# Roots on GpSimd, last squares summed by TensorE, and three kinds of work moved from GpSimd to VectorE

## The chip, the cores and the metric

The kernel runs on one core of one Trainium2 chip. The metric is the device time of that core in microseconds (us), as the median of several executions. The core's engines work side by side, each through a queue of its own in a fixed order: TensorE (PE, matrix products and transposes; PEld is its loading of weights), VectorE (DVE), ScalarE (ACT), GpSimd (POOL) and SyncE (SP, which issues the transfers). An engine that waits for another holds up everything that stands behind the waiting instruction in its queue.

## The reference

Two transformer blocks run one after the other on 256 tokens of width 1024. The second block, which the change touches, has two layers of three sub-layers each (feed-forward, mixer, feed-forward) for two streams: the tokens `h` and a context `hc` of 256 rows, which falls away after the second layer's mixer has read it.

```python
def rms_norm(x, g):
    y = xf * lax.rsqrt(jnp.mean(xf * xf, axis=-1, keepdims=True) + EPS)
    return y.astype(x.dtype) * g
...
    def pre(t, mm, i, gi):
        return rms_norm(t, g[gi]) * (1 + mm[:, :, i + 1]) + mm[:, :, i]

    def post(t, y, mm, i, gi, wres):
        return t + wres * mm[:, :, i + 2] * rms_norm(y, g[gi])

    h = post(h, swiglu(pre(h, m, 0, 0), ffn_wi[0], ffn_wo[0]), m, 0, 1, 0.5)
    hc = post(hc, swiglu(pre(hc, mc, 0, 0), ffn_wi[0], ffn_wo[0]), mc, 0, 1, 0.5)
    u = pre(h, m, 3, 2)
    uc = pre(hc, mc, 3, 2)
```

So between two sub-layers stand two root mean squares: one over the output y, one over the stream after y was added. The first block (a recurrent mixer, a differential attention and two mixtures of experts) is not touched.

## The kernel before

Activations lie transposed: a stream is 8 tiles of 128 channels by 256 tokens (`xT`, `ctxT`). Every product of the second block is made of three TensorE products of halves (`mm3`: high by high, high by low, low by high), so each operand is split into `hi` (ScalarE copy) and `lo` (VectorE subtraction); weights are split as they arrive from memory (`raw`, `hi`, `lo` in `chunks`), inputs in `split_sum`.

A sub-layer ends with 8 output tiles y (index d) per stream. `Output.add` writes for each three squares or products (y squared, gated y squared, gated y by x) into one tile of 128 by 3 by 256: the first is `acc`, the later ones are `ysq`. The tiles d = 1 to 5 are added to `acc` by GpSimd, d = 6 by VectorE, and `acc` and the last tile are then summed over channels by TensorE with a matrix of ones (`sums`, into `st`). `Output.rows` turns `st` into per-token columns (a copy `rowsums`, two TensorE transposes into `tp`, a copy `sums`), and takes the first reciprocal root (`rstd`: a bit trick and two polynomial steps, 11 VectorE instructions on 128 by 2 elements, `rs_x` to `rs_y`). From it and the three sums it works out the squares of the new stream without waiting for it, and takes the second root. Each root is spread over all partitions by two TensorE transposes (`row`). `update` then adds y to the stream (one VectorE product `xs`, one GpSimd addition per tile) and makes the next inputs `u`: a VectorE product, a ScalarE `hi`, and for even tiles a VectorE `lo`, for odd tiles a second ScalarE pass and a GpSimd `lo`.

There are five such boundaries in the second block: after the first feed-forward, the mixer and the second feed-forward of layer 0 and after the first feed-forward of layer 1 for both streams (stream 0 first, stream 1 after it), and after the mixer of layer 1 for stream 0 alone. The last sub-layer (`ffn_last`) has tokens as rows, and takes a root per half of the tokens at the very end. The mixers read a bias, which GpSimd turns round in place (12 subtractions of 128 by 256 per layer).

The code is written in the order of the sub-layers; a scheduler sets the order of each engine's queue from it, so that instructions of stream 1's output, stream 0's update and the next sub-layer stand interleaved.

Of the kernel before, what the change touches and what calls it, by code (L numbers as in the profile page):

```python
# [18 lines left out]
D = 1024  # L19
KT = 8  # L20
# [11 lines left out]
READY = 2  # L32

# [201 lines left out]
class Kernel:  # L235
# [117 lines left out]
    def split_sum(self, hi, lo, src, col, by_pool=False):  # L353

        nc = self.nc
        if by_pool:
            nc.scalar.activation(src, src, AF.Identity, bias=col)
            nc.scalar.activation(hi, src, AF.Copy)
            nc.gpsimd.tensor_sub(lo, src, hi)  # L359
        else:  # L360
            nc.scalar.activation(hi, src, AF.Identity, bias=col)  # L361
            nc.vector.scalar_tensor_tensor(lo, src, col, hi, op0=ALU.add, op1=ALU.subtract)
# [43 lines left out]
    def rstd(self, pool, st, n, dim, tag):  # L406
# [15 lines left out]
        nc.vector.scalar_tensor_tensor(y, t, 1.5, y, op0=ALU.add, op1=ALU.mult)  # L422
        return y
# [54 lines left out]
    class Output:  # L478
# [10 lines left out]
        def add(self, d, s):  # L489
# [10 lines left out]
            if 0 < d < KT - 1:  # L500
                (nc.vector if d == KT - 2 else nc.gpsimd).tensor_add(self.acc[s], self.acc[s], t)  # L501
# [30 lines left out]
        def rows(self, s):  # L532

            kern, nc, pool = self.kern, self.kern.nc, self.pool
            v = pool.tile([128, 3, 2], F32, tag="sums", name="sums", bufs=2)
            t = pool.tile([128, S], F32, tag="xs", name="rowsums", bufs=kern.xs_bufs)[:96]
            nc.vector.tensor_copy(t, self.st[:96, s * S:s * S + S])
# [3 lines left out]
            nc.vector.tensor_copy(v, tp.rearrange("p (j q c) -> p q j c", j=2, q=3)[:, :, :, 0])  # L541
            y2, z2, xz = (v[:, q] for q in range(3))
            x2 = pool.tile([128, 2], F32, tag=f"x2_{s}", name="x2", bufs=2)
            r1 = kern.rstd(pool, y2, 2, D, "n")
            rb1 = kern.row(r1)
            nc.vector.tensor_mul(z2, z2, r1)
            nc.vector.scalar_tensor_tensor(z2, xz, 2.0, z2, op0=ALU.mult, op1=ALU.add)
            nc.vector.tensor_mul(z2, z2, r1)
            nc.vector.tensor_add(x2, self.x2[s], z2)
            self.x2[s] = x2  # L550
            return rb1, kern.row(kern.rstd(pool, x2, 2, D, "n2"))

    def update(self, pool, u, s, out, gs, sh):
# [12 lines left out]
        for k in range(KT):  # L566
# [3 lines left out]
            self.split_sum(u[:, k, 0], u[:, k, 1], t, sh[:, k:k + 1], k % 2)  # L570
# [313 lines left out]
    def mix(self, ring, pool, l, u, out, u_home, proj_home):  # L884
# [974 lines left out]
```

## Time and profile before

| | |
|---|---|
| median of 3 runs | 2648.66 us (2643.46 to 2649.74) |
| the profiled execution's own time | 2648.6 us |
| its span in the trace | 2646.8 us |
| mean granted clock of TensorE | 0.969 |
| busy: PE, PEld, DVE, ACT, POOL | 93%, 72%, 61%, 33%, 13% of the span |
| chain that ended last | PE 58%, DVE 7%, ACT 1%, POOL 0% |

A row of a timeline or a group names the line of the kernel, the engine, the operation and its tiles (out<-in, buffer numbers left out), its size, and in brackets how long the engine sat idle before it and whose end released it. The granted clock is a share of TensorE's full speed of 2.4 GHz; its other level is 1.2 GHz, 0.5. The first block takes about the first 840 us of the span, the second the rest.

### The profile page before, as it was taken

How to read it: one execution, taken by the hardware profiler on the slowest of the kernel's cores; microseconds unless marked ns; L12 is line 12 of the kernel's file. 1: busy time of each engine (PE TensorE's matmuls, PEld its weight loads, DVE VectorE, ACT ScalarE, POOL GpSimd, SP SyncE). 2: the span in 40 equal slices, each digit the busy share in tenths (PEclk: the TensorE clock that was granted, in tenths of full speed). 3: DMA queues.
4: the chain of work that ended last, by engine and by line, in shares of the span. 5: the costliest groups of instructions: out<-in, count | busy, mean ns of one | idle time of the engine just before them, and what ended most of it. 6: DMA issues, size and time to landing. Idle time of an engine off the chain costs nothing.

```text
span 2646.8 us, 38413 instructions
## 1 busy us (share of the span) xinstructions
PE 2457.4 (93%) x14614; PEld 1899.9 (72%) x14614; DVE 1620.8 (61%) x3515; ACT 881.5 (33%) x1547; POOL 340.5 (13%) x364
## 2 busy tenths in 40 slices
PE   4989898988988999998999899999899999898998
PEld 4864344775443888887876788888788888776997
DVE  7873214884131676738847868664868645958555
ACT  3430003551011332224337432223422223455543
POOL 0010000110000000004236500001400002434000
PEclk9989998998999999999999999999999999998999
DMA  9889996789997365622521147443156533322553
GB/s 333 303 351 408 420 419 259 295 292 370 398 410 314 128 199 163 202 89 87 175 64 33 64 152 230 152 158 96 53 188 214 174 119 89 129 79 88 171 180 120
DMA packets 123302, 540.59 MB, mean 204 GB/s; under 512 B 14688, under 2 KB 14944, under 8 KB 98272
## 3 DMA queue, kind: packets, MB, share of 16 engines
q1 hardware_dynamic: 123104, 538.00, 56.4%
q8 instruction: 118, 1.93, 0.3%
q14 instruction: 80, 0.66, 0.1%
HBM read 536.90 MB, written 1.05 MB: 203 GB/s over the span
## 4 chain that ended last, share of the span: by engine, by line
PE 58%; DVE 7%; issue 1%; ACT 1%; POOL 0%; DMA 0%; DVEq 0%; SPq 0%; ACTq 0%; POOLq 0%
PE mm L382 16%; PE mm L383 16%; PE mm L381 16%; DVE lo L374 1%; PE tp L383 1%; PE tp L382 1%; PE tp L381 1%; PE mm L863 1%; PE tp L855 1%; PE mm L843 1%; DVE ysq L499 1%; PE mm L929 1%; PE mm L930 1%; PE mm L928 0%; ACT hi L371 0%
## 5 line engine op out<-in xcount | busy, mean ns | idle before, releaser
L374 DVE TENSOR_TENSOR lo<-raw,hi 128x512 fp32r<-128x512 f32 (+1 forms) x780 | 544.4, 726 | 382.9 <-ACT hi L371 381.1
L371 ACT ACTIVATE hi<-raw 128x1024 fp32r<-128x1024 f32 (+1 forms) x390 | 406.0, 1045 | 891.8 <-PE mm L382 592.8
L381 PE MATMUL mm<-u,hi 128*128 128x512 f32 (+1 forms) x1608 | 574.4, 361 | 16.8 <-ACT hi L371 8.8
L383 PE MATMUL mm<-u,lo 128*128 128x512 f32 (+1 forms) x1608 | 576.5, 360 | 4.7 <-DVE lo L374 4.7
L382 PE MATMUL mm<-u,hi 128*128 128x512 f32 (+1 forms) x1608 | 578.1, 360 | 2.1 <-POOL u L359 1.2
L381 PEld LDWEIGHTS mm<-u,hi 128*128 128x128 f32 x1608 | 308.3, 194 | 63.7 <-ACT u L361 10.8
L383 PEld LDWEIGHTS mm<-u,lo 128*128 128x128 f32 x1608 | 310.7, 193 | 48.9 <-DVE lo L374 6.7
L382 PEld LDWEIGHTS mm<-u,hi 128*128 128x128 f32 x1608 | 311.1, 194 | 46.9 <-POOL u L359 2.7
L382 PE MATMUL mm<-act,hi 128*128 128x512 f32 (+1 forms) x612 | 223.1, 364 | 0.5 <-DVE act L351 0.5
L381 PE MATMUL mm<-act,hi 128*128 128x512 f32 (+1 forms) x612 | 222.3, 363 | 0.0
L383 PE MATMUL mm<-act,lo 128*128 128x512 f32 (+1 forms) x612 | 222.0, 363 | 0.0
L1686 PE MATMUL mm<-raw,xg 128*32 128x512 f32 x1696 | 204.9, 594 | 2.8 <-DMA raw<-in_moe_gu_dram 2.8
L619 DVE SCALAR_TENSOR_TENSOR junk<-raw,conds 128x1024 f32<-128x1024 f32 x128 | 155.5, 1222 | 66.4 <-DMA raw<-in_w_ada_dram 66.2
L619 DVE SCALAR_TENSOR_TENSOR raw<-raw,conds 128x1024 f32<-128x1024 f32 x128 | 156.6, 1229 | 2.4
L1686 PEld LDWEIGHTS mm<-raw,xg 128*32 128x32 f32 x1696 | 63.4, 110 | 119.3 <-issue 108.1
L623 POOL TENSOR_TENSOR mod<-mod,vecs 128x16 f32<-128x16 f32 (+1 forms) x28 | 12.3, 438 | 1029.9 <-DVE raw L619 1000.1
L501 POOL TENSOR_TENSOR acc<-acc,ysq 128x768 f32<-128x768 f32 x45 | 92.5, 2066 | 394.3 <-DVE ysq L499 349.0
L382 PEld LDWEIGHTS mm<-act,hi 128*128 128x128 f32 x612 | 117.6, 192 | 18.8 <-DVE act L351 1.4
L381 PEld LDWEIGHTS mm<-act,hi 128*128 128x128 f32 x612 | 117.3, 192 | 18.9 <-issue 1.2
L383 PEld LDWEIGHTS mm<-act,lo 128*128 128x128 f32 x612 | 117.5, 192 | 17.1
L1718 DVE TENSOR_TENSOR hy<-hy,tp 128x512 f32<-128x512 f32 x56 | 38.1, 686 | 148.2 <-PE tp L1715 147.9
L1686 PE MATMUL mm<-raw,at 128*32 128x512 f32 x880 | 109.7, 594 | 10.3 <-ACT at L1701 8.1
(453 smaller groups left out, 3874.8 us busy)
## 6 DMA issues: line engine op xcount, KB each, us to landing
raw<-in_moe_gu_dram SPq DMA_DIRECT2D x122, 1024.0 KB, 18.1
raw<-in_w_ada_dram SPq DMA_DIRECT2D x200, 512.0 KB, 4.6
raw<-in_ffn_wi_dram SPq DMA_DIRECT2D x176, 512.0 KB, 4.2
raw<-in_moe_down_dram SPq DMA_DIRECT2D x63, 1024.0 KB, 19.8
raw<-in_ffn_wo_dram SPq DMA_DIRECT2D x48, 448.0 KB, 3.8
raw<-in_w_k_dram SPq DMA_DIRECT2D x32, 512.0 KB, 3.6
raw<-in_ffn_wo_dram SPq DMA_DIRECT2D x24, 512.0 KB, 4.3
raw<-in_ffn_wo_last_dram SPq DMA_DIRECT2D x22, 512.0 KB, 3.6
```

Of the source, the lines that this page charges most:

```text
L371: self.mark = self.nc.scalar.activation(hi[:, :m], raw[:, c:c + m], AF.Copy)
L374: self.nc.vector.tensor_sub(lo[:, i:e], raw[:, c + i:c + e], hi[:, i:e])
L381: nc.tensor.matmul(out, lh, rh, start=start, stop=False, skip_group_check=mixed)
L382: nc.tensor.matmul(out, lh, rl, start=False, stop=False, skip_group_check=mixed)
L383: nc.tensor.matmul(out, ll, rh, start=False, stop=stop, skip_group_check=mixed)
L499: nc.vector.scalar_tensor_tensor(t[:, 2], y, self.gate(d, s), kern.xs(d, s), op0=ALU.mult, op1=ALU.mult)
L501: (nc.vector if d == KT - 2 else nc.gpsimd).tensor_add(self.acc[s], self.acc[s], t)
L619: nc.vector.scalar_tensor_tensor(out, rows, 1.0, c, op0=ALU.mult, op1=ALU.mult, accum_out=mod[:, t, s:s + 1])
L843: nc.tensor.matmul(sc[:, :nk], qk[a][half, 512 + t * 128:640 + t * 128], qk[b][half, :nk], start=(i == 0), stop=(i == 2))
L855: nc.tensor.transpose(tp[:, j * 128:j * 128 + 128], p[:, j * 128:j * 128 + 128], self.ident)
L1686: nc.tensor.matmul(ps[t:t + 32], x[:, t:t + 32], w[i][:, s], start=first, stop=last)
L1718: nc.vector.tensor_add(yv, yv, tp)
```

## The change

The reciprocal roots of the second block become one GpSimd instruction each, a power of -0.5 (`rstd2`), with mean and epsilon put in by a VectorE instruction ahead of it. Squares of late tiles are no longer added to `acc` but summed by TensorE directly: from d = 6 on for stream 0 and from d = 4 on for stream 1 (`OWN_SUMS`); the additions that remain are all VectorE's. The copy `rowsums` goes to ScalarE, the three sums are read where the transposes left them. Low parts of odd tiles of `u` and the turning round of the bias go from GpSimd to VectorE; the odd tiles lose their second ScalarE pass.

```diff
+OWN_SUMS = 6, 4
...
-    def split_sum(self, hi, lo, src, col, by_pool=False):
-
-        nc = self.nc
-        if by_pool:
-            nc.scalar.activation(src, src, AF.Identity, bias=col)
-            nc.scalar.activation(hi, src, AF.Copy)
-            nc.gpsimd.tensor_sub(lo, src, hi)
-        else:
-            nc.scalar.activation(hi, src, AF.Identity, bias=col)
-            nc.vector.scalar_tensor_tensor(lo, src, col, hi, op0=ALU.add, op1=ALU.subtract)
+    def split_sum(self, hi, lo, src, col):
+
+        nc = self.nc
+        nc.scalar.activation(hi, src, AF.Identity, bias=col)
+        nc.vector.scalar_tensor_tensor(lo, src, col, hi, op0=ALU.add, op1=ALU.subtract)
...
+    def rstd2(self, x, tag):
+
+        y = self.small.tile([128, 2], F32, tag=tag, name="rp_y", bufs=2)
+        self.nc.gpsimd.tensor_tensor(y, x, self.minus_half, op=ALU.pow)
+        return y
...
-            if 0 < d < KT - 1:
-                (nc.vector if d == KT - 2 else nc.gpsimd).tensor_add(self.acc[s], self.acc[s], t)
+            if 0 < d < OWN_SUMS[s]:
+                nc.vector.tensor_add(self.acc[s], self.acc[s], t)
...
+            if d == OWN_SUMS[s]:
+                self.sums(s, self.acc[s])
+            if d >= OWN_SUMS[s]:
+                self.sums(s, t)
             if d == KT - 1:
-                self.sums(s, self.acc[s])
-                self.sums(s, t)
                 self.done(self, s)
...
-            nc.vector.tensor_copy(t, self.st[:96, s * S:s * S + S])
+            nc.scalar.activation(t, self.st[:96, s * S:s * S + S], AF.Copy)
...
-            r1 = kern.rstd(pool, y2, 2, D, "n")
+            nc.vector.tensor_scalar(m1, y2, 1.0 / D, EPS, op0=ALU.mult, op1=ALU.add)
+            r1 = kern.rstd2(m1, "r1")
             rb1 = kern.row(r1)
-            nc.vector.tensor_mul(z2, z2, r1)
-            nc.vector.scalar_tensor_tensor(z2, xz, 2.0, z2, op0=ALU.mult, op1=ALU.add)
-            nc.vector.tensor_mul(z2, z2, r1)
-            nc.vector.tensor_add(x2, self.x2[s], z2)
-            self.x2[s] = x2
-            return rb1, kern.row(kern.rstd(pool, x2, 2, D, "n2"))
+            nc.vector.reciprocal(inv, m1)
+            nc.vector.scalar_tensor_tensor(w, z2, 1.0 / D, inv, op0=ALU.mult, op1=ALU.mult)
+            nc.vector.tensor_add(w, w, self.x2[s])
+            nc.vector.scalar_tensor_tensor(z, xz, 2.0 / D, r1, op0=ALU.mult, op1=ALU.mult)
+            m2 = kern.small.tile([128, 2], F32, tag=f"x2_{s}", name="x2", bufs=2)
+            nc.vector.tensor_add(m2, w, z)
+            self.x2[s] = m2
+            return rb1, kern.row(kern.rstd2(m2, "r2"))
...
-            self.split_sum(u[:, k, 0], u[:, k, 1], t, sh[:, k:k + 1], k % 2)
+            self.split_sum(u[:, k, 0], u[:, k, 1], t, sh[:, k:k + 1])
...
-            r = self.rstd(pool, sums, 2, D, "n")[:, :1]
+            nc.vector.tensor_scalar(sums, sums, 1.0 / D, EPS, op0=ALU.mult, op1=ALU.add)
+            r = self.rstd2(sums, "r1")[:, :1]
...
-                nc.gpsimd.tensor_sub(bias[:, t, h], self.k("window_up"), bias[:, t, h])
+                nc.vector.tensor_sub(bias[:, t, h], self.k("window_up"), bias[:, t, h])
...
-        self.pre(pool, u, s, self.row(self.rstd(pool, x2, 2, D, "n")), gs[:, :, 0], mod[:, 0:8, 0])
+        self.pre(pool, u, s, self.row(self.rstd(pool, st, 2, D, "n") if s else self.rstd2(x2, "r1")), gs[:, :, 0], mod[:, 0:8, 0])
```

The queues show where the scheduler puts it. On TensorE, at the first boundary, the products of stream 1's last output tile (`mm<-act`) are followed before by its sums, by the transposes of stream 0's second root (`tp<-consts,rs_y`), and by the first products of the next sub-layer (`mm<-u`):

```order
L383 MATMUL mm<-act,lo 128x256
L519 MATMUL st<-acc,consts 32x256 x3
L519 MATMUL st<-ysq,consts 32x256 x3
L427 MATMUL tp<-consts,rs_y 128x128 x2
L381 MATMUL mm<-u,hi 128x256 x4
```

Now the transposes of stream 0's first root (`rp_y`) stand 4 products behind those of `rowsums`, with 52 products `mm<-act` still to come, of which 10 stand ahead of the second root's:

```order
L378 MATMUL mm<-act,hi 128x256
L544 MATMUL tp<-consts,rowsums 128x96 x2
L379 MATMUL mm<-act,hi 128x256
L380 MATMUL mm<-act,lo 128x256
L378 MATMUL mm<-act,hi 128x256
L379 MATMUL mm<-act,hi 128x256
L430 MATMUL tp<-consts,rp_y 128x128 x2
L380 MATMUL mm<-act,lo 128x256
```

What moved: between the two pairs of transposes 27 products stood before and 4 stand now; the second root's transposes moved ahead of stream 1's last two output tiles, and stream 1's last sums moved behind the first 25 products of the next sub-layer.

On VectorE at the same place, the root's steps stand before between tiles of weights (`lo`) and of stream 1's output (`yT`, `ysq`):

```order
L541 COPY sums<-tp 128x6
L412 TENSOR_SCALAR rs_x<-sums 128x2
...
L419 SCALAR_TENSOR_TENSOR rs_y<-rs_t,rs_y 128x2
L710 TENSOR_TENSOR yT<-yT,mm 128x256
L420 TENSOR_TENSOR rs_t<-rs_y 128x2
L499 SCALAR_TENSOR_TENSOR ysq<-yT,gate,ctxT 128x256
L421 TENSOR_TENSOR rs_t<-rs_t,rs_h 128x2
L374 TENSOR_TENSOR lo<-raw,hi 128x512
L422 SCALAR_TENSOR_TENSOR rs_y<-rs_t,rs_y 128x2
```

Now one instruction leads to the first root, and six with the stream's first product and addition between them to the second:

```order
L371 TENSOR_TENSOR lo<-raw,hi 128x512
L548 TENSOR_SCALAR sums<-tp 128x2
L371 TENSOR_TENSOR lo<-raw,hi 128x512
L551 RECIPROCAL sums<-sums 128x2
L568 SCALAR_TENSOR_TENSOR xs<-yT,gate,tp 128x256
L552 SCALAR_TENSOR_TENSOR sums<-tp,sums 128x2
L554 SCALAR_TENSOR_TENSOR sums<-tp,rp_y 128x2
L553 TENSOR_TENSOR sums<-sums,x_0_18388 128x2
L569 TENSOR_TENSOR xT<-xT,xs 128x256
L556 TENSOR_TENSOR x_21120<-sums 128x2
```

What moved: the root's steps are gone from VectorE's queue, and behind these rows follow stream 0's products and low parts for all 8 tiles (22 instructions) before stream 1's last three output tiles are taken up.

GpSimd's queue at the first boundary, before and then now:

```order
L501 TENSOR_TENSOR acc<-acc,ysq 128x768 x10
L562 TENSOR_TENSOR xT<-xT,xs 128x256 x3
L359 TENSOR_TENSOR u<-xs,u 128x256
...
L562 TENSOR_TENSOR ctxT<-ctxT,xs 128x256 x3
...
L899 TENSOR_TENSOR bias<-consts,bias 128x256 x12
```

```order
L425 TENSOR_TENSOR rp_y<-sums,minus_half 128x2
L425 TENSOR_TENSOR rp_y<-x_21120,minus_half 128x2
L569 TENSOR_TENSOR xT<-xT,xs 128x256 x7
L425 TENSOR_TENSOR rp_y<-sums,minus_half 128x2
L425 TENSOR_TENSOR rp_y<-x_21300,minus_half 128x2
L569 TENSOR_TENSOR ctxT<-ctxT,xs 128x256 x7
```

What moved: the additions of squares, the low parts and the bias are gone, and each stream's two powers stand ahead of its seven additions; stream 1's first power stands behind all of stream 0's.

## Rows read from the trace of the kernel before

**Rows 1.** Page, part 1: busy time, share of the span, instructions of each engine.

```profile
PE 2457.4 (93%) x14614; PEld 1899.9 (72%) x14614; DVE 1620.8 (61%) x3515; ACT 881.5 (33%) x1547; POOL 340.5 (13%) x364
```

**Rows 2.** TensorE's waits, 1185 to 2465 us: us in total, times, longest.

```profile
PE tp L427 <- DVE rs_y L422: 22.7, 14, 3.5
PE st L519 <- DVE acc L501: 13.2, 8, 4.3
PE mm L381 <- ACT u L361: 7.8, 7, 1.1
```

**Rows 3.** The five boundaries: stretch, length, busy time of each engine, granted clock, DMA.

```profile
1228.00:1285.00 57.00, 47.43 (x327) 44.26 (x327) 46.80 (x138) 23.95 (x46) 29.90 (x36) 0.88 0.24 83
1484.00:1522.00 38.00, 30.36 (x213) 26.27 (x212) 34.44 (x108) 17.28 (x34) 18.21 (x21) 0.91 0.18 56
1866.00:1915.00 49.00, 39.77 (x276) 36.74 (x276) 38.80 (x120) 21.35 (x43) 20.86 (x24) 0.90 0.14 44
2248.00:2300.00 52.00, 43.71 (x276) 38.31 (x274) 47.84 (x132) 24.34 (x46) 23.51 (x26) 0.90 0.33 118
2428.00:2456.00 28.00, 16.51 (x92) 13.18 (x92) 20.15 (x61) 10.01 (x19) 8.79 (x12) 0.63 0.18 57
```

**Rows 4.** Timeline of TensorE, first boundary: start, us, line, operation, tiles, [idle <-releaser].

```profile
1228.56 0.39 PE L540 MATMUL tp<-consts,rowsums 96*128 96x96 f32 x2
...
1231.91 0.28 PE L381 MATMUL mm<-act,hi 128*128 128x256 f32 x1
1235.18 0.66 PE L427 MATMUL tp<-consts,rs_y 128*128 128x128 f32 x2 [2.98 <-DVE rs_y L422]
...
1241.58 0.63 PE L519 MATMUL st<-acc,consts 128*32 128x256 f32 x6 [1.46 <-DVE acc L501]
1242.04 0.63 PE L519 MATMUL st<-ysq,consts 128*32 128x256 f32 x6
```

**Rows 5.** Timeline of VectorE, last boundary: the two roots of one stream.

```profile
2435.72 0.17 DVE L412 TENSOR_SCALAR rs_x<-sums 128x2 f32<-128x2 f32 x1
...
2437.31 0.16 DVE L422 SCALAR_TENSOR_TENSOR rs_y<-rs_t,rs_y 128x2 f32<-128x2 f32 x1
...
2438.25 0.48 DVE L561 SCALAR_TENSOR_TENSOR xs<-yT,gate,tp 128x256 f32<-128x256 f32 x1 [0.20 <-PE tp L427]
...
2439.18 0.42 DVE L562 TENSOR_TENSOR xT<-xT,xs 128x256 f32<-128x256 f32 x1
...
2441.42 0.16 DVE L422 SCALAR_TENSOR_TENSOR rs_y<-rs_t,rs_y 128x2 f32<-128x2 f32 x1
```

**Rows 6.** Groups of GpSimd, whole span: shapes, count, busy us, mean ns, idle before.

```profile
L501 POOL TENSOR_TENSOR acc<-acc,ysq 128x768 f32<-128x768 f32 x45 | 92.5, 2066 | 394.3 <-DVE ysq L499 349.0 <-DVE lo L374 28.7 <-ACT ysq L498 16.4
L359 POOL TENSOR_TENSOR u<-xs,u 128x256 fp32r<-128x256 f32 x36 | 28.2, 783 | 8.0 <-ACT u L358 7.9
L899 POOL TENSOR_TENSOR bias<-consts,bias 128x256 f32<-128x256 f32 x24 | 19.0, 827 | 2.7 <-DMA bias<-in_rpb_dram 2.7
L623 POOL TENSOR_TENSOR mod<-mod,vecs 128x8 f32<-128x8 f32 x12 | 4.1, 342 | 340.6 <-DVE raw L619 310.9 <-DVE hy L619 26.8 <-DVE rs_y L419 2.9
```

**Rows 7.** Groups of VectorE, 1185 to 2647 us.

```profile
L501 DVE TENSOR_TENSOR acc<-acc,ysq 128x768 f32<-128x768 f32 x9 | 8.6, 954 | 0.5
```

**Rows 8.** Timelines of VectorE and GpSimd in the last mixer's output tiles.

```profile
2409.23 1.29 DVE L374 TENSOR_TENSOR lo<-raw,hi 128x512 fp32r<-128x512 f32 x2
...
2414.72 2.94 DVE L374 TENSOR_TENSOR lo<-raw,hi 128x512 fp32r<-128x512 f32 x2
2417.58 0.41 DVE L984 COPY yT<-mm 128x256 f32<-128x256 f32 x1
2418.10 0.48 DVE L499 SCALAR_TENSOR_TENSOR ysq<-yT,gate,xT 128x256 f32<-128x256 f32 x1
...
2415.19 1.92 POOL L501 TENSOR_TENSOR acc<-acc,ysq 128x768 f32<-128x768 f32 x1 [0.67 <-ACT ysq L498]
```

**Rows 9.** Timeline of VectorE, first boundary: inputs of stream 0, and after stream 1's.

```profile
1249.17 0.48 DVE L561 SCALAR_TENSOR_TENSOR xs<-yT,gate,tp 128x256 f32<-128x256 f32 x1
1249.56 0.48 DVE L569 SCALAR_TENSOR_TENSOR xs<-xT,gs,tp 128x256 f32<-128x256 f32 x1
...
1278.27 1.06 DVE L374 TENSOR_TENSOR lo<-raw,hi 128x512 fp32r<-128x512 f32 x1 [6.16 <-ACT hi L371]
```

**Rows 10.** Timeline of VectorE at the program's end.

```profile
2636.64 0.17 DVE L412 TENSOR_SCALAR rs_x<-sums 128x2 f32<-128x2 f32 x1
...
2642.32 1.42 DVE L784 SCALAR_TENSOR_TENSOR yg<-yg,rs_y,rows 128x512 f32<-128x512 f32 x2
```

More of the change, by code (lines that the diff above doesn't have):

```diff
@@ L534, in rows @@
             kern, nc, pool = self.kern, self.kern.nc, self.pool
-            v = pool.tile([128, 3, 2], F32, tag="sums", name="sums", bufs=2)
             t = pool.tile([128, S], F32, tag="xs", name="rowsums", bufs=kern.xs_bufs)[:96]
-            nc.vector.tensor_copy(t, self.st[:96, s * S:s * S + S])
+            nc.scalar.activation(t, self.st[:96, s * S:s * S + S], AF.Copy)
             tp = kern.tp()[:, :192]
@@ L540, in rows @@
                 nc.tensor.transpose(tp[:, 96 * j:96 * j + 96], t[:, j * 128:j * 128 + 128], kern.ident[:96, :96])
-            nc.vector.tensor_copy(v, tp.rearrange("p (j q c) -> p q j c", j=2, q=3)[:, :, :, 0])
-            y2, z2, xz = (v[:, q] for q in range(3))
-            x2 = pool.tile([128, 2], F32, tag=f"x2_{s}", name="x2", bufs=2)
-            r1 = kern.rstd(pool, y2, 2, D, "n")
-            rb1 = kern.row(r1)
-            nc.vector.tensor_mul(z2, z2, r1)
-            nc.vector.scalar_tensor_tensor(z2, xz, 2.0, z2, op0=ALU.mult, op1=ALU.add)
-            nc.vector.tensor_mul(z2, z2, r1)
-            nc.vector.tensor_add(x2, self.x2[s], z2)
-            self.x2[s] = x2
-            return rb1, kern.row(kern.rstd(pool, x2, 2, D, "n2"))
+            y2, z2, xz = (tp.rearrange("p (j q c) -> p q j c", j=2, q=3)[:, q, :, 0] for q in range(3))
+            v = kern.small.tile([128, 4, 2], F32, tag="sums", name="sums", bufs=2)
+            m1, inv, w, z = (v[:, i] for i in range(4))
+            nc.vector.tensor_scalar(m1, y2, 1.0 / D, EPS, op0=ALU.mult, op1=ALU.add)
+            r1 = kern.rstd2(m1, "r1")
+            rb1 = kern.row(r1)
+            nc.vector.reciprocal(inv, m1)
[6 more added lines that the diff above has]
+            return rb1, kern.row(kern.rstd2(m2, "r2"))
     def update(self, pool, u, s, out, gs, sh):
@@ L772, in ffn_last @@
                 down(f, j)
-            sums = pool.tile([128, 3, 2], F32, tag="sums", name="sums", bufs=2)[:, 0]
+            sums = self.small.tile([128, 4, 2], F32, tag="sums", name="sums", bufs=2)[:, 0]
             t = pool.tile([128, D], F32, tag="pt", name="yg", bufs=2)
@@ L1000, in second_block @@
             pool.tile([128, n], F32R if tag == "act" else F32, tag=tag, name=tag, bufs=b)
+        self.small = pool
         ready, mark = {}, None
@@ L1027, in enter @@
             self.update(pool, u[s], s, out, gs[:, :, s], mod[:, i * 8:(i + 1) * 8, s])
+        self.minus_half = pool.tile([128, 2], F32, name="minus_half")
+        nc.gpsimd.memset(self.minus_half, -0.5)
         with self.tc.issue_after(mark.ins):
@@ L1053, in start @@
         x2 = self.x2[s] = self.cp.tile([128, 2], F32, name=f"x2_{s}")
-        self.nc.vector.tensor_copy(x2, self.x_squares(pool, s))
+        st = self.x_squares(pool, s)
+        self.nc.vector.tensor_scalar(x2, st, 1.0 / D, EPS, op0=ALU.mult, op1=ALU.add)
         mod = self.mod2[0][:, :, s:s + 1]
```

## The prediction, made before the changed kernel was run

> **What bounds the kernel now.** I read the page's busy times first: TensorE is busy 93% of the span, no other engine over 72% [rows 1], so time is won where TensorE waits or runs at its lower clock. The waits of TensorE over the second block's boundaries name three causes that this change touches: 22.7 us for the last step of a root, 13.2 us for VectorE's addition to `acc`, 7.8 us for the first high part of the next inputs [rows 2]. Then the five boundaries by themselves: length less busy time is 9.6, 7.6, 9.2, 8.3 and 11.5 us, together 46 us, and the granted clock there is 0.88 to 0.91 and once 0.63 [rows 3]. A mean clock c over W us means (1-c)W of work lost to the lower level (1.2 GHz): 6.8, 3.4, 4.9, 5.2 and 10.4 us. At the last boundary the low clock covers 2 x 10.4 = 21 us, of which some 11.5 were idle anyway, so only about 4.6 us are lost; in all some 25 us. About 70 us (2.6%) is all that could be won here.
>
> The timeline of the first boundary shows how a wait arises. The transposes of `rowsums` run at 1228.56, 27 products follow until 1231.91, then TensorE sits for 2.98 us until stream 0's first root is there at 1235.18 [rows 4]. The root took over 6 us because its 11 steps stood between other work in VectorE's queue; undisturbed, at the last boundary, the same steps take from 2435.72 to 2437.47, 1.75 us [rows 5].
>
> **What a power costs.** No row shows one. Below, it can't be cheaper than a small GpSimd instruction, 0.34 us for 128 by 8 [rows 6]. Above, I take the 1.75 us of VectorE's steps times the ratio of the engines on one addition, 2066 to 954 ns or 2.2 [rows 6, 7]: 3.8 us. I take 0.9 us, nearer to the small instruction, since it is one instruction on two columns, with half a microsecond for the steps of a power inside it, and 0.2 us for the hand-overs to and from GpSimd (VectorE waited 0.20 us for TensorE's transposes at 2438.25 [rows 5]): 1.1 us for a root.
>
> The Trainium skill speaks against it: GPSIMD Engine Reference, section Engine selection, keeps elementwise work on VectorE because GpSimd takes about twice as long. The 2.2 above agrees with it. A root done as a chain at that rate costs the upper bound, and the sum then changes sign; that is the second rival.
>
> **A boundary with two streams, after the change.** A product of 256 columns takes 0.12 us (27 in 3.3 us [rows 4]).
> - Stream 0's first root: mean and epsilon 0.17 us, half of a `lo` of 0.69 ahead of it, root 1.1, less 4 products of cover (0.5): TensorE waits 1.1 us, where it waited 3.0.
> - Its second root: product 0.48, four small steps of 0.16, addition 0.42 [rows 5] and root 1.1, 2.6 us in all, less 10 products, the root's transposes and a sum (1.6): 1.0 us.
> - Stream 1's last tiles: VectorE now serves stream 0's 22 instructions first, which start 0.39 us apart [rows 9]: 8.7 us, and 1 us for meetings with GpSimd; then about 2.4 us for stream 1's outputs and products. TensorE has 42 + 25 + 10 products and 11 sums (10.1 us). It waits 2.0 us, at its sums. This wait is new, and takes the place of those for `acc` and for the first high part.
> - `rowsums` on ScalarE against 4 products: 0.2 us. Stream 1's roots: 0.17 + 0.35 + 1.1 less 7 products, 0.8 us; 2.6 less 13 products, 1.0 us. What is queued behind each is the next sub-layer's products, so none of it is hidden.
>
> Together 6.1 us. Gaps of one or two us instead of three should bring the clock down less: 1.5 us taken, between 0 and the 5 of before. TensorE also gets 12 more sum products (3 for stream 0, 9 for stream 1), 6 of which start in 0.46 us [rows 4]: 0.9 us. So 8.5 us stay per boundary, against (34.7 idle + 20.3 clock)/4 = 13.75 before. Gain 5.25 each, **21 us for four**. The low parts of odd tiles lengthen VectorE's work by 4 x 0.39 us per stream, within the 22 instructions above; TensorE's 12 products per tile (1.4 us) are slower than VectorE's 1.2 us per tile, which hides it.
>
> **The last boundary (one stream).** Here VectorE is late before the sums: with GpSimd's addition beside it, two `lo` take 2.94 instead of 1.29 us [rows 8], so a tile costs 0.41 + 0.48 + 2.94 = 3.8 us against TensorE's 24 products, 2.9 us. That makes the longest wait for `acc`, 4.3 us [rows 2]. With VectorE's own addition (0.95 [rows 7]) in its place the tile costs 3.1 us, for five tiles: lag of about 1 us, gain 3.3. The first root takes 0.17 + 1.1 instead of about 1.9 with its copy: 0.65. From the first product to the end of the second root 2.6 instead of 3.3 us (2438.25 to 2441.58 [rows 5]): 0.7. `rowsums` not behind `lo`: 0.5; clock 1. Against it 0.8 for odd low parts, which the next products, 6 a tile, don't hide, and 0.2 for sums. **Gain 5.**
>
> **The rest.** The bias: 12 subtractions of some 0.42 us, 5 us on VectorE in each of two mixers. They fall where VectorE sat idle for 6.16 us [rows 9], but now late low parts and stream 1 press on the same place, and a `lo` of the next weights stands behind them: 1.5 us each, **-3**, between 0 and -10. The end: the two roots in a row took from 2636.64 to 2643.74, 7.1 us [rows 10]; now 2 x (0.17 + 1.1 + 1.4) + 1.3 + 0.2 = 6.8: **0.3**. The start's root has 4 products of cover and costs about a microsecond, which the wait for weights after it takes up: 0. In the feed-forwards' wide tiles VectorE gives 0.95 us per moved addition and gets back the 1.65 it lost beside GpSimd; TensorE doesn't wait there: 0.
>
> **Sum.** 21 + 5 - 3 + 0.3 = 23 us. The profiled execution took 2648.6 us (its span 2646.8), the same as the median of 2648.66, so **2626 us**.
>
> **Rivals.** (1) *Everything hides.* The power costs 0.34 us: 0.56 us less for each of 20 roots (four at each of four boundaries, two at the last, two at the end) gives 11 us more; with a full clock (6) and no wait for stream 1's sums (8) at best 2602. For it: the small GpSimd row. Against: VectorE's queue at the boundary.
>
> (2) *The power is slow.* At 3.8 us each of these 20 roots costs 2.9 us more, 58 us, and the clock falls as before (6): 2690, slower. Each microsecond of the power costs 20 us; from 2.05 us on the gain is gone, and from 2.4 the kernel is slower. No row excludes it.
>
> (3) *VectorE gives it back.* The bias costs its 10 us in full (7 more), the wait for stream 1's sums doubles (8), the odd low parts show (4): 2645, no change. For it: VectorE's busy 47 of 57 and 48 of 52 us at two boundaries [rows 3]. Against: 18 roots leave its queue, some 25 us, and the stretching beside GpSimd goes.
>
> (4) *The first power loads code.* A first execution that stops GpSimd for 6 us would be paid once, at the start, where 0.5 us of products cover it: 2632. No row shows such a stop. The Trainium skill has that rule in GPSIMD Engine Reference, section Instruction dispatch: the first call to freshly loaded code pays about 6 us.
>
> **Chances.** The forecast, 2608 to 2640, 0.53; the first rival 0.10; the fourth 0.05; the third 0.16; the second 0.16. A change within 0.3% (8 us) is about what a measurement of this kernel can't tell from none. Faster 0.68 (forecast, first and fourth), same 0.16, slower 0.16. The range reaches from the full hiding to a power of 2.4 us: 2602 to 2656; the forecast's own is 2608 to 2640.
>
> **What will show it.** The power's row on GpSimd at 0.4 to 1.5 us, 21 times (one at the start); TensorE's waits at `rp_y` of about a microsecond, four per boundary; at each two-stream boundary a wait for `ysq` where those for `acc` and the first high part were; the granted clock of the five stretches above 0.95, the last above 0.75; two `lo` at 1.3 us beside the last mixer's output tiles. The prediction is wrong if the power takes over 2 us, or if VectorE's queue, with bias and stream 0's tiles ahead of stream 1's, starves TensorE behind the roots.

## The result, and the profile of the changed kernel

The changed kernel takes **2619.51 us** (median of 4 runs, 2617.38 to 2622.59), the kernel before beside it on the same chip 2646.78 us. The ratio is **0.9898, 95% interval 0.9884 to 0.9912**: 27 us faster. The forecast was 2626, range 2602 to 2656, so time and sign were right. The way there was not: the experiments show that the roots gave 10 to 12 us, the additions and sums some 24, and that the low parts took some 7 back.

The profiled execution took 2618.24 us (span 2616.5, mean granted clock 0.978, before 0.969). The page's first part, busy time of each engine, answers to [rows 1]: TensorE's work is the same, GpSimd's fell from 340 to 219 us, VectorE's from 1621 to 1574 although it took over three kinds of work.

```profile
PE 2460.2 (94%) x14716; PEld 1891.1 (72%) x14716; DVE 1574.3 (60%) x3373; ACT 866.5 (33%) x1521; POOL 219.3 (8%) x281
```

The groups of GpSimd show the powers (shapes, count, busy us, mean ns, idle before): 21 of them, 0.69 us for a second root, 0.95 for a first.

```profile
L425 POOL TENSOR_TENSOR rp_y<-sums,minus_half 128x2 f32<-128x2 f32 x11 | 10.4, 945 | 676.7 <-DVE sums L548 488.6 <-DVE sums L788 188.1
L425 POOL TENSOR_TENSOR rp_y<-x,minus_half 128x2 f32<-128x2 f32 x10 | 6.9, 691 | 26.6 <-DVE x L556 13.7 <-DVE x L1066 11.0 <-PE mm L380 1.8
```

TensorE's waits from 1185 to 2440 us (total, times, longest) answer to [rows 2]. The 22.7 us for roots became 11.1, the 13.2 for `acc` are gone, and of the 7.8 for the first high part 1.9 stay. Where stream 1's sums now stand there is only 0.9.

```profile
PE tp L430 <- POOL rp_y L425: 11.1, 17, 1.4
PE mm L851 <- ACT p L825: 4.7, 4, 2.3
PE mm L378 <- ACT u L358: 1.9, 4, 1.1
PE mm L379 <- DVE u L359: 1.7, 4, 0.6
...
PE st L524 <- DVE ysq L502: 0.9, 3, 0.3
PE tp L544 <- ACT rowsums L541: 0.7, 2, 0.5
```

The five boundaries by themselves (stretch, length, busy time of each engine, granted clock, DMA), as in [rows 3]. The granted clock is at its upper level throughout in three of them; at the fourth it is 0.93, before 0.90, and at the last 0.86, before 0.63. Length less busy time is 4.1, 2.8, 3.0, 3.9 and 4.8 us, together 18.7, where it was 46.

```profile
1220.50:1275.00 54.50, 50.38 (x378) 42.40 (x373) 42.87 (x112) 22.21 (x44) 14.52 (x18) 1.00 0.23 78
1475.00:1512.00 37.00, 34.20 (x265) 28.89 (x264) 31.38 (x78) 18.23 (x36) 14.60 (x18) 1.00 0.13 43
1851.00:1895.00 44.00, 40.99 (x314) 34.84 (x312) 32.45 (x83) 18.05 (x36) 14.15 (x18) 1.00 0.15 49
2226.00:2274.00 48.00, 44.12 (x288) 35.90 (x287) 40.30 (x107) 20.66 (x39) 13.97 (x18) 0.93 0.27 93
2405.00:2430.00 25.00, 20.16 (x140) 16.95 (x139) 18.91 (x44) 12.27 (x23) 7.01 (x9) 0.86 0.24 84
```

**A clock for comparing profiles.** The transposes of `rowsums` are found in every version, nine times (two streams at four boundaries, one at the last). Their start times cut each execution into nearly the same pieces of the program; the scheduler shifts some products past these marks, so before two pieces are compared their products have to be counted. Before, the first stands at 1228.6 us [rows 4]; of the changed kernel the second is this row of TensorE's timeline:

```profile
1244.89 0.38 PE L544 MATMUL tp<-consts,rowsums 96*128 96x96 f32 x2
```

| piece, us | before | changed | difference |
|---|---|---|---|
| start to the first mark | 1228.6 | 1225.4 | -3.2 |
| stream 0's mark to stream 1's, boundary 1 | 24.9 | 19.5 | -5.4 |
| the same, boundary 2 | 24.0 | 17.4 | -6.6 |
| the same, boundary 3 | 25.3 | 19.9 | -5.4 |
| the same, boundary 4 | 24.8 | 19.6 | -5.2 |
| stream 1's mark to the next stream 0's, four together | 1107.3 | 1108.0 | +0.7 |
| last mark to the end | 211.9 | 206.7 | -5.2 |

From the first mark to the last it is 21.9 us, and 5.2 us behind the last: the gain stands at the boundaries, where it was looked for. How it divides between the short pieces and the long ones is less sure than the table looks. Between the marks TensorE now runs 18 products of the next sub-layer fewer (25 at the second boundary) and 18 records of stream 1's sums more (a product of these sums is two records in the trace); these shifts are worth some 4 of the 22.6 us, and the long pieces took the shifted products up without growing. The first piece is no evidence: among the profiles below it lies between 1222.4 and 1237.3 us, with no pattern that follows the edits. So pieces are read behind the first mark only, and verdicts from the timed runs.

### The profile page after: what moved, and what is told of

It reads as the page before. It is cut to its first block, busy times and chain, and to the rows that moved or that the text cites. A ratio compares the mean times of both kernels' runs of the same rounds, so it can differ in the third digit from the quotient of the medians.

```text
span 2616.5 us, 38380 instructions
## 1 busy us (share of the span) xinstructions
PE 2460.2 (94%) x14716; PEld 1891.1 (72%) x14716; DVE 1574.3 (60%) x3373; ACT 866.5 (33%) x1521; POOL 219.3 (8%) x281
## 4 chain that ended last, share of the span: by engine, by line
PE 62%; DVE 3%; POOL 1%; ACT 1%; issue 1%; POOLq 0%; DVEq 0%; ACTq 0%
PE mm L378 17%; PE mm L380 17%; PE mm L379 17%; PE tp L380 1%; PE tp L379 1%; PE tp L378 1%; PE mm L871 1%; PE tp L863 1%; PE mm L851 1%; PE st L524 1%; POOL rp_y L425 1%; PE mm L936 1%; PE mm L937 1%; PE mm L938 1%; DVE u L359 1%
## 5 line engine op out<-in xcount | busy, mean ns | idle before, releaser
L371 DVE TENSOR_TENSOR lo<-raw,hi 128x512 fp32r<-128x512 f32 (+1 forms) x780 | 513.2, 686 | 374.3 <-ACT hi L368 372.2
L378 PEld LDWEIGHTS mm<-u,hi 128*128 128x128 f32 x1608 | 305.0, 190 | 59.8 <-ACT hi L368 10.5
L380 PEld LDWEIGHTS mm<-u,lo 128*128 128x128 f32 x1608 | 305.3, 190 | 53.2 <-DVE lo L371 8.6
L379 PEld LDWEIGHTS mm<-u,hi 128*128 128x128 f32 x1608 | 305.9, 190 | 45.8 <-DVE u L359 3.3
L1708 DVE TENSOR_TENSOR xn<-xn,mm 128x512 f32<-128x512 f32 x14 | 9.6, 688 | 176.8 <-PE mm L1698 164.1
L626 DVE SCALAR_TENSOR_TENSOR raw<-raw,cond 128x1024 f32<-128x1024 f32 x88 | 105.9, 1226 | 9.7 <-ACT sq L462 9.5
```

The lines of the kernel that those rows point to most:

```text
L371: self.nc.vector.tensor_sub(lo[:, i:e], raw[:, c + i:c + e], hi[:, i:e])
L378: nc.tensor.matmul(out, lh, rh, start=start, stop=False, skip_group_check=mixed)
L379: nc.tensor.matmul(out, lh, rl, start=False, stop=False, skip_group_check=mixed)
L380: nc.tensor.matmul(out, ll, rh, start=False, stop=stop, skip_group_check=mixed)
L626: nc.vector.scalar_tensor_tensor(out, rows, 1.0, c, op0=ALU.mult, op1=ALU.mult, accum_out=mod[:, t, s:s + 1])
```

## The experiments

Each was timed beside the kernel before (0.9898 is the changed kernel). One per cent is 26.5 us. Ratios from different chips are compared, so differences of 2 or 3 us between runs are not read.

| run | median us | ratio | interval |
|---|---|---|---|
| roots back on VectorE | 2629.54 | 0.9943 | 0.9932 to 0.9955 |
| additions of squares on GpSimd | 2628.39 | 0.9938 | 0.9926 to 0.9950 |
| TensorE's late sums taken back | 2627.55 | 0.9930 | 0.9917 to 0.9943 |
| low parts of odd tiles on GpSimd | 2611.81 | 0.9873 | 0.9859 to 0.9888 |
| bias on GpSimd | 2619.30 | 0.9902 | 0.9888 to 0.9916 |
| roots alone, all else as before | 2635.25 | 0.9963 | 0.9950 to 0.9976 |
| three powers per root | 2636.92 | 0.9965 | 0.9952 to 0.9978 |
| low parts of stream 0 on GpSimd | 2615.16 | 0.9897 | 0.9880 to 0.9914 |
| low parts of stream 1 on GpSimd | 2616.16 | 0.9885 | 0.9868 to 0.9901 |
| low parts on GpSimd, own sums from 6 and 2 | 2620.40 | 0.9896 | 0.9878 to 0.9914 |
| low parts on GpSimd, own sums from 5 and 3 | 2620.10 | 0.9910 | 0.9892 to 0.9927 |

**The theory** was the prediction's sum: mainly the roots leave VectorE's queue, the rest is small, low parts and bias hide. **The rival**: VectorE's queue at the boundary is what counts, so whatever lengthens it ahead of stream 1's squares costs, and whatever leaves it gains.

### The roots

Undone alone:

```diff
     def rstd2(self, x, tag):
-        y = self.small.tile([128, 2], F32, tag=tag, name="rp_y", bufs=2)
-        self.nc.gpsimd.tensor_tensor(y, x, self.minus_half, op=ALU.pow)
-        return y
+        return self.rstd(self.small, x, 2, 1, "n" if tag == "r1" else "n2")
```

> The changed kernel with its roots taken on VectorE again (the 11 steps; all else as changed, so additions of squares, low parts and bias stay on VectorE). The prediction's account (the short root is most of the gain): TensorE's waits at the roots' transposes go from 11 us back to over 20 us and the clock falls at the boundaries again, some 15 us lost of the 27 gained, ratio to before 0.994 to 0.997. Rival (the gain comes from GpSimd's additions no longer standing in VectorE's way): under 5 us lost, ratio 0.990 to 0.992.

Taking the roots back costs 0.45%, 11.9 us. The time is within what was expected, the way is not: TensorE's waits at the roots' transposes, 1185 to 2450 us, stay at 11.2 us in all, where over 20 were expected. They are fewer and longer.

```profile
PE tp L428 <- DVE rs_y L419: 11.2, 5, 3.3
PE mm L378 <- ACT u L358: 5.8, 6, 1.6
```

Of the 11.2 us 5.4 stand at the last boundary and 5.8 at stream 1's roots; at stream 0's roots of the two-stream boundaries TensorE doesn't wait. The wait for the next inputs' first high part rises from 1.9 to 5.8 us. Behind the first mark the pieces add up to 8.0 us more than the changed kernel's, 4.5 of them behind the last mark. Between the marks the scheduler puts 20 products more than in the changed kernel (over 35 at the second boundary), so these pieces by themselves aren't compared.

Put in alone (additions, low parts and bias on GpSimd as before, `acc` and the last tile summed by TensorE as before; the new small steps and the copy on ScalarE go with the roots):

```diff
-OWN_SUMS = 6, 4
+OWN_SUMS = 7, 7
...
-                nc.vector.tensor_add(self.acc[s], self.acc[s], t)
+                (nc.vector if d == KT - 2 else nc.gpsimd).tensor_add(self.acc[s], self.acc[s], t)
...
+            nc.gpsimd.tensor_sub(lo, src, hi)
...
+                nc.gpsimd.tensor_sub(bias[:, t, h], self.k("window_up"), bias[:, t, h])
```

> The kernel before with one part of the change alone: the second block's roots as GpSimd powers, with the rowsums copy on ScalarE and the shorter chain of small steps that goes with them. Additions of squares, low parts of odd tiles and the bias stay on GpSimd, and TensorE sums acc and the last tile. If the roots give here what taking them back cost (11 us), the ratio is 0.9955. If GpSimd's additions and low parts stand ahead of a power in GpSimd's queue, less is gained, or nothing: 0.998 to 1.00.

The roots alone give 0.37%, 9.8 us. Both ways round they are worth 10 to 12 us, less than half of the whole. What stays without the other parts is again in TensorE's waits, 1185 to 2450 us: 14.3 us for GpSimd's low parts and 6.3 for `acc`.

```profile
PE mm L384 <- POOL u L361: 14.3, 11, 3.3
PE tp L435 <- POOL rp_y L430: 13.2, 15, 1.7
PE st L529 <- DVE acc L509: 6.3, 7, 3.7
```

The price of a power was tested by lengthening it:

```diff
+        z = self.small.tile([128, 2], F32, tag=tag + "z", name="rp_z", bufs=2)
+        self.nc.gpsimd.tensor_tensor(z, x, self.minus_half, op=ALU.pow)
+        self.nc.gpsimd.tensor_tensor(z, z, self.minus_half, op=ALU.pow)
         self.nc.gpsimd.tensor_tensor(y, x, self.minus_half, op=ALU.pow)
```

> The changed kernel with two more powers on GpSimd ahead of each root, whose results nobody uses, so that each root takes about 1.4 us longer (two rows of 0.69). If every microsecond of the power costs the 20 us that the prediction took, the time rises by 28 us: 2648, ratio 1.00. If half the roots are covered by other products, it rises by some 14 us: 2634, ratio 0.995. If the roots are hidden, it stays at 0.990.

The edit did less to a root than its code says. The scheduler put only one of the two added powers ahead of the root (`rp_y`, L428); the other stands behind it in GpSimd's queue. GpSimd's timeline at the first boundary, second root of stream 0:

```profile
1241.41 0.69 POOL L426 TENSOR_TENSOR rp_z<-x,minus_half 128x2 f32<-128x2 f32 x1 [1.10 <-DVE x L559]
1242.07 0.69 POOL L428 TENSOR_TENSOR rp_y<-x,minus_half 128x2 f32<-128x2 f32 x1
1242.72 0.69 POOL L427 TENSOR_TENSOR rp_z<-rp_z,minus_half 128x2 f32<-128x2 f32 x1
```

So each of 20 roots comes some 0.65 us later, not 1.4, and the expectation's cases don't apply as they stand. TensorE's waits at the roots' transposes, 1185 to 2460 us, double from 11.1 to 22.9 us, 0.65 us for each of 18 roots. Behind the first mark the pieces are longer by 5.0 us between the two streams of the four boundaries, 4.9 ahead of the next, and 3.5 behind the last: 13.4 us for 20 times 0.65, so by the pieces the delay is paid in full, and a microsecond of the power costs some 20 us. The timed runs show 0.67%, 17.7 us. The power behind the root, which stands ahead of the stream's additions, is in both figures; whether it costs anything by itself was not tested.

```profile
PE tp L433 <- POOL rp_y L428: 22.9, 18, 2.1
```

### The additions and the sums

Additions on GpSimd, TensorE's late sums kept:

```diff
-                nc.vector.tensor_add(self.acc[s], self.acc[s], t)
+                nc.gpsimd.tensor_add(self.acc[s], self.acc[s], t)
```

> The changed kernel with its additions of squares (d up to 5 for stream 0, up to 3 for stream 1) on GpSimd again. The prediction's account: VectorE's low parts take 2.9 instead of 1.3 us a pair again beside the last mixer's output tiles, VectorE is late there by 3 to 4 us, and the same at the first mixer's end; elsewhere TensorE doesn't wait; 5 to 8 us lost, ratio 0.992 to 0.993. Rival (the additions were the cause at all five boundaries): 12 us or more lost, ratio over 0.994.

It costs 0.40%, 10.6 us, more than expected. The waits for `acc` are back, and the pieces ahead of stream 0's marks are longer, by 0.2, 1.4, 1.4 and 2.6 us; between the two streams' marks nothing moves.

```profile
PE st L524 <- POOL acc L504: 5.3, 4, 1.5
```

The other half, additions on VectorE but up to the sixth tile of both streams:

```diff
-OWN_SUMS = 6, 4
+OWN_SUMS = 7, 7
```

> The changed kernel, but the squares of tiles 1 to 6 of both streams are added on VectorE and TensorE sums only acc and the last tile, as before the change: 12 sum products a boundary fewer on TensorE, four additions of 0.95 us a boundary more on VectorE (one for stream 0, three for stream 1). If the late sums on TensorE matter only by their 0.9 us, the time is 3 us lower a run (ratio 0.989). If stream 1's squares would queue on VectorE behind stream 0's next inputs, each two-stream boundary is 2 to 4 us longer: 2628 to 2636, ratio 0.993 to 0.996, with waits of the sums for acc.

It costs 0.32%, 8.5 us, as the second expectation had it: TensorE's waits, 1185 to 2440 us, for `acc` and for the next inputs' parts return, and the pieces between the marks are longer by 2.4, 3.8, 2.2 and 2.5 us. Ahead of the marks of the second and third boundary 3.3 and 3.4 us are won back: there TensorE has six records of sums fewer, which at the price of [rows 4] is 0.5 us, so most of it stays open.

```profile
PE mm L379 <- DVE u L359: 5.7, 15, 0.6
PE st L524 <- DVE acc L504: 5.3, 4, 1.7
```

Each half undone costs 8 to 11 us. Both together can be read from two runs: the one with the low parts on GpSimd differs from the one with the roots alone by additions, sums and bias, and is 0.90% or 23.8 us faster, and by the pieces behind the first mark 24.3 us; the bias by itself measures nothing (below). **Additions and sums together are worth 24 us**, the larger part of the change.

### The low parts and the bias

```diff
-            self.split_sum(u[:, k, 0], u[:, k, 1], t, sh[:, k:k + 1])
+            self.split_sum(u[:, k, 0], u[:, k, 1], t, sh[:, k:k + 1], k % 2)
```

> The changed kernel with the low parts of odd tiles of the next inputs on GpSimd again (and their second ScalarE pass). The prediction's account: the low parts are hidden behind TensorE's 1.4 us a tile at four boundaries and cost 0.8 us at the last, so the time is that of the changed kernel within 2 us, ratio 0.989 to 0.991. Rival (GpSimd's path was the slower one, and made stream 1's root wait behind it): 4 us or more lost, ratio 0.992 or more.

This version is **faster than the changed kernel**: 2611.81 us, ratio 0.9873, by 0.25% or 6.6 us; the run with the bias put back, on the same chip, took 2619.30. The waits at the roots are the same 11.1 us. What differs is VectorE's timeline at the first boundary. In the changed kernel, from stream 0's product of its second tile, which follows the steps of its second root, to stream 1's first square behind it:

```profile
1228.63 0.48 DVE L568 SCALAR_TENSOR_TENSOR xs<-yT,gate,tp 128x256 f32<-128x256 f32 x1
...
1238.34 1.29 DVE L359 SCALAR_TENSOR_TENSOR u<-xs,mod,u 128x256 fp32r<-128x256 f32 x3 [0.19 <-ACT u L358]
1239.54 0.48 DVE L576 SCALAR_TENSOR_TENSOR xs<-xT,gs,tp 128x256 f32<-128x256 f32 x1
1239.93 0.48 DVE L502 SCALAR_TENSOR_TENSOR ysq<-yT,gate,ctxT 128x256 f32<-128x256 f32 x1
...
1245.31 0.16 DVE L548 TENSOR_SCALAR sums<-tp 128x2 f32<-128x2 f32 x1 [1.24 <-PE tp L544]
```

and with the low parts of odd tiles on GpSimd:

```profile
1230.53 0.48 DVE L573 SCALAR_TENSOR_TENSOR xs<-yT,gate,tp 128x256 f32<-128x256 f32 x1
...
1240.22 0.48 DVE L581 SCALAR_TENSOR_TENSOR xs<-xT,gs,tp 128x256 f32<-128x256 f32 x1 [0.22 <-POOL xT L574]
1240.61 0.48 DVE L507 SCALAR_TENSOR_TENSOR ysq<-yT,gate,ctxT 128x256 f32<-128x256 f32 x1
...
1245.45 0.16 DVE L553 TENSOR_SCALAR sums<-tp 128x2 f32<-128x2 f32 x1 [0.23 <-PE tp L549]
```

Stream 1's first square starts 11.30 us behind that product in the one, 10.08 in the other; its `sums` come 16.68 and 14.92 us behind. The four odd low parts (0.54 us each) had lengthened VectorE's stretch ahead of stream 1 by 1.2 us, and stream 1's root came 1.8 later. The two runs that move one stream's low parts separate the places:

```diff
+            self.split_sum(u[:, k, 0], u[:, k, 1], t, sh[:, k:k + 1], k % 2 and s == 0)
```

> The changed kernel, but the low parts of the odd tiles of stream 0 alone are on GpSimd again (at the last two boundaries and the start as the stream there is numbered). All odd tiles on GpSimd gave 7 us. If the cost of VectorE's low parts is that stream 0's tiles delay stream 1's outputs and squares, which stand behind them in VectorE's queue, nearly the whole 7 us come back: ratio 0.987 to 0.988. If each low part costs where its own tile is awaited, half comes back or less: 0.9885 to 0.989.

```diff
+            self.split_sum(u[:, k, 0], u[:, k, 1], t, sh[:, k:k + 1], k % 2 and s == 1)
```

> The other half of the run before it: the changed kernel with the low parts of the odd tiles of stream 1 alone on GpSimd again. If the cost of VectorE's low parts is that stream 0's tiles stand ahead of stream 1's outputs and squares, nothing moves between stream 0's second and stream 1's first root (it shortened by 1.7 to 2.1 us at three boundaries with stream 0's low parts on GpSimd), and the time is that of the changed kernel within 2 us: ratio 0.989 to 0.990. If the low parts cost where their own tile is awaited, it is 3 to 4 us faster: 0.988 to 0.9885.

By their times they are inconclusive: the intervals 0.9880 to 0.9914 and 0.9868 to 0.9901 hold both what was expected and the changed kernel. Their pieces are plain. Between the marks of the two streams, against the changed kernel:

| low parts of odd tiles on GpSimd | boundary 1 | 2 | 3 | 4 |
|---|---|---|---|---|
| both streams | -1.7 | +0.9 | -2.0 | -1.7 |
| stream 0 | -1.7 | +0.9 | -2.0 | -1.7 |
| stream 1 | 0.0 | 0.0 | -0.3 | 0.0 |

So stream 0's low parts delay stream 1, stream 1's do not, at three boundaries of four; at the second it is the other way round, for a reason that stays open. These pieces add up to 4.5 us of the 6.6; the rest lies in the long pieces, where the run with stream 0 alone differs by -2.1 to +3.0 us and the profiles scatter as much, and isn't attributed.

```diff
-                nc.vector.tensor_sub(bias[:, t, h], self.k("window_up"), bias[:, t, h])
+                nc.gpsimd.tensor_sub(bias[:, t, h], self.k("window_up"), bias[:, t, h])
```

> The changed kernel with the bias turned round on GpSimd again. The prediction's account: the 12 subtractions press on VectorE behind stream 1's inputs in each of two mixers and cost 1.5 us each, so this is 3 us faster than the changed kernel, ratio 0.988 to 0.989. Rival (they fall in VectorE's idle time): no difference, ratio 0.990; a gain from the move would show as 0.991 or more.

No difference: 2619.30 against 2619.51. VectorE's 24 subtractions take 0.42 us each and nothing waits for them.

### Further on the faster version

```diff
-OWN_SUMS = 6, 4
+OWN_SUMS = 6, 2
```

> The version with the low parts of odd tiles on GpSimd, and from tile 2 instead of tile 4 on TensorE sums stream 1's squares itself: at each two-stream boundary two additions of 0.95 us fewer on VectorE and six sum products more on TensorE. If stream 1's squares are still late behind stream 0's inputs, some 1 us a boundary is gained: ratio 0.985 to 0.986. If they no longer are, the products cost 0.7 us a boundary: 0.988 to 0.989.

```diff
-OWN_SUMS = 6, 4
+OWN_SUMS = 5, 3
```

> The version with the low parts of odd tiles on GpSimd, and TensorE sums the squares itself one tile earlier in both streams (from tile 5 and tile 3). It differs from the run with tiles 6 and 2 by stream 0's fifth tile: if VectorE's additions are late there too, above all at the last boundary, it is faster than that run by up to 2 us; if not, slower by 0.5 us a boundary, some 2 us.

Both lose what the low parts had given: 0.9896 and 0.9910 for 0.9873, though the first one's interval still touches that of the version they start from. Between the marks the pieces are those of the version they start from to 0.2 us, so nothing more is to be had from stream 1's squares; ahead of stream 0's marks they are longer by 0.6 to 3.6 us. TensorE's timeline of the first of the two runs, ahead of the first mark, shows three sums of stream 1 (`acc` and tiles 2 and 3) that now stand ahead of the three of stream 0:

```profile
1212.59 0.63 PE L529 MATMUL st<-acc,consts 128*32 128x256 f32 x6
1213.05 0.61 PE L529 MATMUL st<-ysq,consts 128*32 128x256 f32 x6
1216.29 0.63 PE L529 MATMUL st<-ysq,consts 128*32 128x256 f32 x6
...
1229.79 0.33 PE L549 MATMUL tp<-consts,rowsums 96*128 96x96 f32 x2
```

In the changed kernel, with the limits 6 and 4, stream 1's `acc` is summed between the transposes of stream 0's two roots, beside TensorE's waits for them:

```profile
1227.10 0.43 PE L430 MATMUL tp<-consts,rp_y 128*128 128x128 f32 x2 [0.91 <-POOL rp_y L425]
...
1228.64 0.62 PE L524 MATMUL st<-acc,consts 128*32 128x256 f32 x2
```

In the profiles the first run pays 7.7 us in these pieces, some 2 us a boundary. Its page counts 12 records of sums more a boundary, 0.9 us at the price of [rows 4]; why it is twice that stays open. Of the three placings tried, 6 and 4 has the lowest time, and the version with the low parts on GpSimd has the lowest median of the study.

## Why the prediction came out right, and where its steps were wrong

**What bounds the kernel.** Right: the gain is where TensorE waited, 21.9 us from the first mark to the last and 5.2 behind it, against 21 and 5 in the sum.

**The power.** Right: 0.69 to 0.95 us for the 0.9 taken, so the second rival (a slow power, 3.8 us) falls, with the bound that came from the engines' ratio. The fourth rival, a first power that loads code, shows nothing: the first one, at 872.92 us, took 0.70. The Trainium skill's rule in GPSIMD Engine Reference, section Instruction dispatch, of about 6 us for the first call to freshly loaded code is not seen at this instruction; whether its code had been loaded earlier, no run here shows.

**What a microsecond of it costs.** Right as far as the run shows: by the pieces 13.4 us for 0.65 us more at each of 20 roots, 20 us for a microsecond. By the timed runs' 17.7 us it would be 27, and the third power is in both.

**The waits at the roots.** Mis-sized, too large. The prediction left 3.9 us of them at each two-stream boundary and some 2 at the last, 17 to 18 in all; 11.1 are recorded, of 22.7 before [rows 2]. But these waits are no measure of the roots: with the roots alone they are 13.2 us and 9.8 us are gained, and with the roots alone taken back they are 11.2 and 11.9 us are lost. Then the loss stands behind the last mark and in other waits.

**Stream 1's sums.** Mis-sized the other way about: the waits for `acc` and the first high part, 13.2 and 7.8 us before [rows 2], were to be replaced by 2.0 us a boundary at `ysq`; 0.9 us in all are recorded there. Additions and sums, which take those waits away, are worth 24 us, more than the roots.

**What stays at a boundary.** Its three terms were mis-sized, and cancel. By the prediction's reckoning 8.5 us were to stay at each of the four boundaries: 6.1 of waits, 1.5 of clock and 0.9 for the added sums. Length less busy time leaves 13.8 us there, 3.5 each, and the one stretch with a granted clock of 0.93 another 3.4, 0.9 each. So waits and clock gained 38 us (55 less 17.2), where the sum had 25.

The added sums took back more than was put for them. The prediction counted 12 products a boundary and priced them by the profile's records, 6 in 0.46 us [rows 4]. But each of these products is two records: the page counts 102 more (14716 for 14614), which is 24 at each of the four boundaries and 6 at the last. And they don't run six in a row, since stream 1's squares reach TensorE one by one. TensorE's timeline of the changed kernel has two of them alone, which hold it for 0.55 us until the next product:

```profile
1240.47 0.62 PE L524 MATMUL st<-ysq,consts 128*32 128x256 f32 x2 [0.29 <-DVE ysq L502]
1241.02 0.51 PE L378 MATMUL mm<-u,hi 128*128 128x256 f32 x2
```

TensorE's busy time on these sums alone, between the two marks of the first boundary (stretch, length, busy time of PE and PEld, granted clock, DMA), is 1.09 us for 12 before, 5.08 for 30 in the changed kernel and 4.23 for 30 with the low parts on GpSimd:

```profile
1228.56:1253.50 24.94, 1.09 (x12) 0.44 (x12) 0.86 0.32 106
1225.35:1244.89 19.54, 5.08 (x30) 1.38 (x30) 1.00 0.15 30
1227.25:1245.03 17.78, 4.23 (x30) 1.31 (x30) 1.00 0.10 30
```

From the first mark to the last it is 12.6 us for 96 before and 26.4 for 192 now, some 14 us more, or 12 if each group is counted to the next product's start. That is 3 us a boundary or more, not 0.9. So 38 us less 12 to 14 should be gained, 24 to 26, and the pieces show 21.9; the stretches of before and after don't hold the same products, and where the last 2 to 4 us are stays open. The sums' time counts as busy time, and no wait names it; the prediction took a cost to be where the trace would name a wait.

VectorE's stretch ahead of stream 1, which the prediction put at 9.7 us, is 11.3 (above). With the low parts on GpSimd it is 10.1, and the sums of the row above are shorter by 0.85 us: part of what the low parts cost is time of these sums.

**Low parts of odd tiles.** Wrong: taken as hidden, they cost 6.6 us by the timed runs. The prediction weighed them against TensorE's 12 products a tile; what they delay isn't their own tile but stream 1's squares behind them in VectorE's queue, as the pieces show at three boundaries of four; the timed runs of the two halves are too close to confirm it. This was in the third rival, at 4 us.

**The bias.** Wrong by its 3 us: it costs nothing.

**The last boundary.** The sum of 5 us and 0.3 for the end came out, 5.2 us behind the last mark, but not from its terms. Of them 3.3 us were for the lag at `acc` and 0.5 for `rowsums`, both ahead of the mark; behind it stood 0.65 and 0.7 for the roots, 1 for the clock and 0.3 for the end, less 0.8 for low parts, some 2 us. Two runs show that nearly all of the 5.2 us are the roots': with the roots alone this piece is 207.0 us, of 211.9 before, and with the roots alone taken back it is 211.1. VectorE's timeline shows the chain from the mean to the second power without anything between:

```profile
2410.23 0.16 DVE L548 TENSOR_SCALAR sums<-tp 128x2 f32<-128x2 f32 x1 [0.98 <-PE tp L544]
...
2411.69 0.48 DVE L568 SCALAR_TENSOR_TENSOR xs<-yT,gate,tp 128x256 f32<-128x256 f32 x1 [0.26 <-PE tp L430]
2412.09 0.15 DVE L556 TENSOR_TENSOR x<-sums 128x2 f32<-128x2 f32 x1
```

and GpSimd's the second power itself:

```profile
2412.32 0.69 POOL L425 TENSOR_TENSOR rp_y<-x,minus_half 128x2 f32<-128x2 f32 x1 [1.15 <-DVE x L556]
```

From the stream's first product to the end of the second root it takes 1.32 us (2411.69 to 2413.01), where the prediction had 2.6 and before it was 3.33 [rows 5]. That is 2.0 us for the 0.7 in the sum. The 16.1 us ahead of the last mark have TensorE busy for 15.25, before for 11.28, with a granted clock of 1.00 for 0.84; the wait of 4.3 us for `acc` that was to go is not there any more:

```profile
2393.80:2409.90 16.10, 15.25 (x129) 13.71 (x128) 14.89 (x26) 9.70 (x18) 0.00 (x0) 1.00 0.59 191
```

The whole piece between the marks of boundaries 4 and 5 is no shorter, though (161.2 us, before 160.7). It holds 27 products more (995 records for 968), among them 18 shifted past stream 1's mark, which at 0.12 us are some 2 us; where the rest of the lag's 3.3 us went stays open.

So the sum was right by errors that cancel, which is luck: the waits and the clock that stay were put 13 us too high, the sums 8 to 10 us too low, the low parts' 6.6 us were taken as hidden, the roots at the last boundary were worth more than was put and the lag at `acc` less, and the bias was put 3 us too dear.

## What to carry to other kernels

Where several kinds of work feed one queue, price an edit by what stands behind the moved instructions in that queue, not by the wait of their own reader, and undo each part alone before crediting it; an engine that gets its inputs one by one looks busy. An engine that is idle 92% of the time is the right place for small work that others stand in line behind (these low parts), even if it does it slower. Look where the scheduler put an added instruction before reading its run: of two powers meant to lengthen a root, one landed behind it. Cutting two executions at the same instruction gives pieces that can be compared to a microsecond or two, when total times scatter by more, once the products in them are counted.

## What the runs showed of the hardware

A power on 128 by 2 elements takes GpSimd 0.69 us. It takes 1.01 to 1.08 us when it starts while VectorE runs a `lo` of 128 by 512, a subtraction of two inputs, as all eight first roots of the two-stream boundaries do. At the first boundary, of the changed kernel, GpSimd's and VectorE's timelines:

```profile
1225.96 1.08 POOL L425 TENSOR_TENSOR rp_y<-sums,minus_half 128x2 f32<-128x2 f32 x1 [138.53 <-DVE sums L548]
1225.80 0.68 DVE L371 TENSOR_TENSOR lo<-raw,hi 128x512 fp32r<-128x512 f32 x1
```

At the last boundary, with only small steps on VectorE, the first power takes 0.70 us. In the run with the roots alone stream 0's first powers have no `lo` beside them and take 0.69 to 0.70 us, stream 1's have one and take 1.08. A `lo` that starts after the power doesn't lengthen it: stream 1's second powers in the changed kernel have one beside them for 0.46 to 0.55 us and take 0.69.

Even two columns on GpSimd meet VectorE's large subtractions, as `lo` met the large additions before [rows 8]. The Trainium skill, GPSIMD Engine Reference, section Specifications, has the two engines' memory interfaces shared, with contention where VectorE reads two inputs; the rows of the first powers agree, and those of stream 1's second powers show an overlap that costs the power nothing.
